# ScalarE evacuates the adaLN product banks, M6 becomes the last product of a feed-forward, and a fifth load buffer replaces two slots

## The chip, the cores and the metric

One core of a Trainium2 chip runs the whole kernel. The metric is the device time of one execution in microseconds; lower is better. The times shown are of several executions, and one further execution was recorded by the hardware profiler.

## The reference

A trunk of two layers over 512 tokens with 1024 channels. Each layer has three sub-layers: a SwiGLU feed-forward, a token mixer (mLSTM in layer 0, Mamba-2 in layer 1) and a second feed-forward. Every sub-layer is wrapped in the same way, with a shift, a scale and a gate that come from a conditioning vector (adaLN):

```python
def swiglu(h, w1, w3, w2):
    return (jax.nn.silu(h @ w1) * (h @ w3)) @ w2

def sublayer(x, fn, g_pre, g_post, shift, scale, gate, weight):
    hmod = rms_norm(x, g_pre) * (1 + scale[:, None, :]) + shift[:, None, :]
    y = rms_norm(fn(hmod), g_post)
    return x + weight * gate[:, None, :] * y

# per layer i
mod = (c_act @ ada_w[i] + ada_b[i]).reshape(B, N_SUB, 3, D_MODEL)
```

All of it is float32, and d_ff is 2816 (22 tiles of 128).

## The kernel before, in words

**Products in three matmuls.** TensorE multiplies in a reduced float32 format, so each operand is split into a high part (ScalarE copy, L174 or L191) and a low part (VectorE subtraction, L175 or L192), and each product is three matmuls (`mm3`, L186 to L188).

**Loads.** Weights come through `raw` tiles of 128x1024 floats from the pool `rawp`, which has four buffers. SyncE issues these loads in order. A `raw` is free again when its low part has been computed, which in turn writes into one of three `wl` buffers, whose reader is TensorE. Loads of weights stand on L162 (`unit`), of adaLN's weights on L203, of the feed-forward's second matrix on L713 (`blocks`), and of pieces for the late products on L723 (`behind`).

**Slots.** All other activations live in 52 tiles of 128x512 floats (`Slots`), taken first freed, first used. A taken slot carries a wait for the last reader of what it held. A `raw` buffer is as large as two slots. Counted through the program, the fewest free slots at any `get` are 3, at the end of three of the feed-forwards (names `kl`, `v`, and once `grow` in the first of them); in the Mamba mixer the fewest are 4.

**Feed-forward.** `first` and `rest` run over the 22 tiles of d_ff; each tile is two projections into PSUM banks `mm0` and `mm1`, silu on ScalarE (L598) and a product on VectorE (L599). Pairs of tiles give factors for a fast (Strassen-like) second product with seven half-size products M1 to M7. `flush` runs M5, M1 and M7 as the stream goes, and stores three combinations of weight blocks to DRAM from GpSimd (`w2s`, L688). `outp` then runs M3, M4, and two rows of token tiles last: before, M6 and then M2, the last three groups of which are kept in slots (`hold`, L191 and L192) so that one token tile ends before the other. M6 enters one half (`hi`) of the rows of token tiles 2 and 3, M2 enters both halves, one of them subtracted. `Post.evac` squares and gates a half, `Post.finish` does the norm, the residual and the next sub-layer's input (or, after the last sub-layer, the store of the output).

**adaLN beside it.** In the streams of the feed-forwards, `pump` runs steps of adaLN: a load of 128x1024 weights and a multiply-add on VectorE (L208). When a sum is ready, `settle` runs `columns` (shift and scale: 24 narrow matmuls, bank read at L233) or `gate_rows` (gate: two matmuls at L252 for each of two halves, bank read by VectorE at L254, which also adds the row loaded at L249). They take an `aux` bank if one is free and otherwise an `mm` bank in turn; all six `gate_rows` of the program take `mm0` and `mm1`, the same that the next tile of the stream needs. VectorE and ScalarE each run their instructions in one order, laid out when the kernel is built.

Of the kernel before, what the change touches and what calls it, by code (L numbers as in the profile page):

```python
# [12 lines left out]
AF = mybir.ActivationFunctionType  # L13
ALU = mybir.AluOpType
# [4 lines left out]
ND = D // P  # L19
# [16 lines left out]
HELD = 3  # L36
# [11 lines left out]
START_A = 1  # L48
START_X = (2,3)
START_S = 4  # L50
N_SLOTS = 52
ADA_END = 20
ADA_R = (2.6,2.25,2.25,1)

# [2 lines left out]
def trunk(ctx: ExitStack, tc: tile.TileContext, i: dict, out: bass.AP):  # L57
    nc = tc.nc
    pool = lambda name, bufs=1, **k: ctx.enter_context(tc.tile_pool(name=name, bufs=bufs, **k))
# [2 lines left out]
    hmp = pool("hmp", 16)  # L62
    ygp = pool("ygp", 4)
    slp = pool("slp")
    rawp = pool("rawp", 4)
    whp = pool("whp", 3)
    wlp = pool("wlp", 3)
    accp = pool("accp", 1)
# [4 lines left out]
    act = nc.scalar.activation  # L73
    tt = nc.vector.tensor_tensor
# [20 lines left out]

    slots, banks = Slots(slp, "s", N_SLOTS), Slots(aux, "a", 4)

    def slot(dt=F32, name="sl", cols=T):
        return slots.get(dt, name, cols)
# [5 lines left out]
    def ps_mm(k=None):  # L105

        if k is None:
            k = mm_turn[mm_next[0] % len(mm_turn)]
            mm_next[0] += 1
        return mm.tile([P, T], F32, tag=f"mm{k}", name="mm")  # L110

    def ps_aux():
        return banks.get(F32, "aux")
# [3 lines left out]
    def ps_ada():  # L117

        if banks.free_:
            ps = ps_aux()  # L120
            return ps, lambda: done_ps(ps)
        return ps_mm(), lambda: None


    def load_const(name):
        ap = i[name]
        t = const.tile(list(ap.shape), F32, name="c_" + name)
        nc.sync.dma_start(t, ap)
        return t
# [5 lines left out]
    ada_b = load_const("ada_b")  # L135
# [48 lines left out]
    def mm3(ps, stat, mov, first, last):  # L184

        matmul(ps, stat[0], mov[0], start=first, stop=False)  # L186
        matmul(ps, stat[0], mov[1], start=False, stop=False)  # L187
        matmul(ps, stat[1], mov[0], start=False, stop=last)  # L188

    def split(dst_h, dst_l, src):  # L190
        act(dst_h, src, AF.Copy)  # L191
        tt(dst_l, src, dst_h.bitcast(F32), ALU.subtract)  # L192
# [5 lines left out]
    def ada_kind(l, s, kind):  # L198
        st = {}

        def step(kc):
            raw = rawp.tile([P, 1024], F32, tag="raw", name="raw")
            nc.sync.dma_start(raw, i["ada_w"][l * 9 + s * 3 + kind - 2, kc])  # L203
            if kc == 0:
                st["acc"] = accp.tile([P, 1024], F32, tag="acc", name="acc")
                ts(st["acc"], raw, csil[:, 0:1], None, ALU.mult)
            else:
                stt(st["acc"], raw, csil[:, kc:kc + 1], st["acc"], ALU.mult, ALU.add)  # L208
            if kc == ND - 1:
                acc = st["acc"]  # L210
                if kind == 2:
                    parts = []
                    for c in range(2):
                        parts.append((slot(F32R, "adah"), slot(F32R, "adal")))
                        split(*parts[c], acc[:, c * T:(c + 1) * T])
                    ready.append(lambda: gate_rows(parts))
                else:
                    parts = [slot(BF16, "adas", 1024) for _ in range(3)]
                    act(parts[0], acc, AF.Copy)
                    tt(acc, acc, parts[0], ALU.subtract)  # L220
                    act(parts[1], acc, AF.Copy)
                    tt(parts[2], acc, parts[1], ALU.subtract)
                    ready.append(lambda: columns(parts))

        def columns(parts):
            ps, done = ps_ada()
            for j in range(ND):
                for q in range(3):
                    matmul(ps[:, j:j + 1], parts[q][:, j * P:(j + 1) * P], ones_b, start=q == 0, stop=q == 2)
            n0 = (l * 3 + s) * ND  # L230
            c0 = kind * DEPTH * NSUB * ND + n0
            r = const.tile([P, ND], F32, name=f"mod{l}{s}{kind}")
            tt(r, ps[:, :ND], ada_b[:, c0:c0 + ND], ALU.add)  # L233
            free(*parts)
            done()
            if kind == 0:
                SH[l, s] = r
            else:
                stt(r, r, 1.0, n_pre[:, n0:n0 + ND], ALU.add, ALU.mult)
                A[l, s] = r  # L240

        def gate_rows(parts):

            G[l, s] = []
            for c in range(2):
                rows = []
                for name in ("gate_b", "norm_post"):
                    rows.append(slot(name="row"))
                    nc.sync.dma_start(rows[-1], i[name][l * 3 + s:l * 3 + s + 1, c * T:(c + 1) * T].to_broadcast([P, T]))  # L249
                ps, done = ps_ada()  # L250
                for q, t in enumerate(parts[c]):
                    matmul(ps, ones_r, t, start=q == 0, stop=q == 1)  # L252
                g = slot(name="grow")
                tt(g, ps, rows[0], ALU.add)  # L254
                stt(g, g, 0.5 if s != 1 else 1.0, rows[1], ALU.mult, ALU.mult)
                G[l, s].append(g)
                free(*rows, *parts[c])
                done()
        for kc in range(ND):
            adaq.append(lambda kc=kc: step(kc))  # L260

# [271 lines left out]
    class Ffn:  # L533
# [207 lines left out]
        def outp(self, nxt):  # L741
            n = NF // 2
            groups = [range(j, min(j + 2, n)) for j in range(0, n, 2)]
            lo, hi = slice(0, T), slice(T, D)
            m3 = [ps_mm(0), ps_mm(1)]
            for js in groups[:3]:
                self.sums(m3, 3, js)
            while self.pairs or self.pending:
                self.step()
            post = Post(self.l, self.sub, nxt)  # L750
            m, yg = self.m, post.yg
            for t in range(2):
                act(yg[2 + t][:, hi], m[1][t], AF.Copy)
                act(yg[t][:, hi], m[5][t], AF.Copy)
                tt(yg[t][:, lo], yg[2 + t][:, hi], m[7][t], ALU.add)
                tt(yg[t][:, lo], yg[t][:, lo], yg[t][:, hi], ALU.add)
            done_ps(*m[1], *m[5])
            for js in groups[3:]:
                self.sums(m3, 3, js)
            for t in range(2):  # L760
                tt(yg[t][:, hi], m3[t], yg[t][:, hi], ALU.subtract)
                tt(yg[2 + t][:, hi], yg[2 + t][:, hi], m3[t], ALU.add)
                post.evac(t, 1, yg[t][:, hi])

            m4 = [ps_aux(), ps_aux()]
            for js in groups:
                self.sums(m4, 4, js)
                for j in js:
                    free(*self.kept[j]["34"])
            for t in range(2):  # L770
                tt(yg[t][:, lo], yg[t][:, lo], m4[t], ALU.add)
                act(yg[2 + t][:, lo], m4[t], AF.Copy)
            done_ps(*m4)
            for t in range(2):
                post.evac(t, 0, yg[t][:, lo])
                post.finish(t)

            m6 = [ps_mm(2), ps_mm(3)]
            for js in groups:
                self.sums(m6, 6, js)  # L780
            for t in range(2):
                tt(yg[2 + t][:, hi], yg[2 + t][:, hi], m6[t], ALU.add)

            m2, held = [ps_mm(0), ps_mm(1)], {}
            for js in groups[:-HELD]:
                self.sums(m2, 2, js)
                for j in js:
                    free(*self.kept[j]["62"])
            for js in groups[-HELD:]:
                held.update(zip(js, self.hold(2, js)))  # L790
            for t in range(2):
                c = slice(t * P, (t + 1) * P)
                for j in held:
                    ah, al = self.kept[j][2]
                    mm3(m2[t], (ah[:, c], al[:, c]), held[j], False, j == n - 1)
                    if t:
                        free(*self.kept[j]["62"], *held[j])
                u = 2 + t
                tt(yg[u][:, lo], yg[u][:, lo], m2[t], ALU.add)
                post.evac(u, 0, yg[u][:, lo])  # L800
                tt(yg[u][:, hi], yg[u][:, hi], m2[t], ALU.subtract)
                post.evac(u, 1, yg[u][:, hi])
                post.finish(u)
            mm_turn[:] = [0, 1, 2, 3]
            return post
# [472 lines left out]
    ps = [[ps_mm(), ps_mm()], [ps_mm(), ps_mm()], p2]  # L1278
# [46 lines left out]
    post = f00.outp((0, 1))  # L1325
# [18 lines left out]
    post = Post(0, 1, (0, 2))  # L1344
# [3 lines left out]
    post = f01.outp((1, 0))  # L1348
# [3 lines left out]
    post = f10.outp((1, 1))  # L1352
# [19 lines left out]
    post = Post(1, 1, (1, 2), mb.yacc)  # L1372
# [91 lines left out]
```

## Time and profile before

| | us |
|---|---|
| median of three runs | 2104.86 |
| the three runs | 2102.46 to 2107.49 |
| the profiled execution, its own time | 2103.91 |
| the profiled execution, span from first to last instruction | 2102.1 |

TensorE is busy for 2043.4 us of the span (97%), VectorE for 1618.5 (77%), ScalarE for 1004.0 (48%), GpSimd for 83.2 (4%). The mean granted clock of TensorE is 0.993 of full speed. A busy TensorE is no proof that it runs at its peak: the granted clock of a stretch says at which of its two levels (1.2 and 2.4 GHz) it ran, 1.00 being all of it at the higher. In an idle row, the name behind the arrow is what the engine waited for last.

### The profile page before, as it was taken

The page shows a single profiled execution, that of the slowest core. Times are in us where ns is not written, and L with a number is a line of the kernel's source. Part 1 is how long each engine was busy: PE and PEld are TensorE (multiplying, and loading weights), DVE is VectorE, ACT ScalarE, POOL GpSimd, SP SyncE. Part 2 cuts the span into 40 slices and gives each one's busy share as a digit, 9 for nine tenths or more (in the row PEclk, how much of TensorE's full clock was granted, in tenths as well). Part 3 has the DMA queues.
Part 4 walks back from the last instruction along what each step waited for, and adds up shares of the span by engine and source line. Part 5 has one row for each costly group of instructions (what it writes and reads, how often), then busy time and mean ns, then how long its engine had stood idle before and what let it go on. Part 6 is the DMA issues. An engine that isn't in the chain of part 4 may idle for free.

```text
span 2102.1 us, 28333 instructions
## 1 busy us (share of the span) xinstructions
PE 2043.4 (97%) x10422; PEld 1704.5 (81%) x10422; DVE 1618.5 (77%) x2687; ACT 1004.0 (48%) x1721; POOL 83.2 (4%) x165
## 2 busy tenths in 40 slices
PE   7999999999999999899999999999999999999998
PEld 5887778898789788788977788888887789878886
DVE  8979977858986888668768787889898758575666
ACT  5434335645564343347533334765665645333344
POOL 0001000000000000000000000000000000000000
PEclk9999999999999999999999999999999999999999
DMA  7567775445424677745467675533433334454454
GB/s 275 184 200 244 261 244 187 137 146 157 138 79 156 204 262 243 229 153 173 156 221 264 211 232 180 168 127 118 131 96 120 121 111 131 165 180 147 157 163 155
DMA packets 124604, 369.17 MB, mean 176 GB/s; under 512 B 15081, under 2 KB 15081, under 8 KB 124465
## 3 DMA queue, kind: packets, MB, share of 16 engines
q1 hardware_dynamic: 113904, 332.75, 49.4%
q0 software_dynamic: 10560, 34.61, 4.3%
q8 instruction: 81, 1.33, 0.3%
q14 instruction: 59, 0.48, 0.1%
HBM read 330.46 MB, written 36.85 MB: 175 GB/s over the span
## 4 chain that ended last, share of the span: by engine, by line
issue 48%; PE 34%; DVE 8%; DMA 6%; ACT 3%; POOL 1%; SPq 0%; POOLq 0%; DVEq 0%; ACTq 0%
PE mm L186 9%; PE mm L188 9%; PE mm L187 9%; DMA raw<-in_w 3%; PE aux L186 2%; PE aux L188 2%; PE aux L187 2%; DMA raw<-in_ada_w 2%; DVE wl L192 1%; POOL w2s L688 1%; DVE wl L175 1%; ACT wh L174 1%; DVE acc L208 1%; DVE tl L192 0%; DVE kl L192 0%
## 5 line engine op out<-in xcount | busy, mean ns | idle before, releaser
L186 PE MATMUL mm<-hm,wh 128*128 128x512 f32 (+1 forms) x2128 | 775.4, 367 | 13.1 <-DVE grow L254 6.6
L188 PE MATMUL mm<-hm,wl 128*128 128x512 f32 (+1 forms) x2128 | 772.1, 364 | 11.2 <-DVE wl L175 11.2
L187 PE MATMUL mm<-hm,wh 128*128 128x512 f32 (+1 forms) x2128 | 773.0, 364 | 0.0
L186 PEld LDWEIGHTS mm<-hm,wh 128*128 128x128 f32 x2128 | 402.7, 190 | 81.5 <-ACT wh L174 9.8
L188 PEld LDWEIGHTS mm<-hm,wl 128*128 128x128 f32 x2128 | 403.9, 190 | 78.7 <-DVE wl L175 16.4
L187 PEld LDWEIGHTS mm<-hm,wh 128*128 128x128 f32 x2128 | 404.4, 190 | 61.9 <-issue 2.0
L174 ACT ACTIVATE wh<-raw 128x1024 fp32r<-128x1024 f32 (+1 forms) x294 | 278.3, 957 | 360.1 <-PE mm L187 125.5
L175 DVE TENSOR_TENSOR wl<-raw,wh 128x1024 fp32r<-128x1024 f32 (+1 forms) x294 | 319.3, 1098 | 88.1 <-ACT wh L174 85.4
L191 ACT ACTIVATE wh<-raw 128x1024 fp32r<-128x1024 f32 (+1 forms) x172 | 158.2, 920 | 281.0 <-PE mm L187 146.4
L192 DVE TENSOR_TENSOR wl<-raw,wh 128x1024 fp32r<-128x1024 f32 (+1 forms) x172 | 179.9, 1048 | 50.4 <-ACT wh L191 49.0
L208 DVE SCALAR_TENSOR_TENSOR acc<-raw,csil,acc 128x1024 f32<-128x1024 f32 x112 | 143.8, 1284 | 75.3 <-DMA raw<-in_ada_w 74.9
L599 DVE TENSOR_TENSOR s<-s,mm 128x512 f32<-128x512 f32 (+1 forms) x97 | 59.8, 619 | 87.4 <-PE mm L188 87.1
L191 ACT ACTIVATE kh<-s 128x256 fp32r<-128x256 f32 x132 | 54.4, 412 | 86.0 <-DVE s L599 75.5
L186 PE MATMUL mm<-wh,kh 128*128 128x512 f32 x224 | 87.7, 392 | 0.0
L187 PE MATMUL mm<-wl,kh 128*128 128x512 f32 x224 | 87.5, 391 | 0.0
L188 PE MATMUL mm<-wh,kl 128*128 128x512 f32 x224 | 87.3, 390 | 0.0
L688 POOL DMA_DIRECT2D w2s<-v x44 | 24.0, 546 | 1392.9 <-DVE v L680 922.2
L186 PE MATMUL aux<-wh,th 128*128 128x512 f32 x176 | 68.6, 391 | 0.9 <-ACT wh L191 0.8
L187 PE MATMUL aux<-wl,th 128*128 128x512 f32 x176 | 68.4, 390 | 0.5 <-DVE wl L192 0.5
L188 PE MATMUL aux<-wh,tl 128*128 128x512 f32 x176 | 68.3, 389 | 0.0
L680 DVE TENSOR_TENSOR v<-raw 128x512 f32<-128x512 f32 x44 | 30.3, 690 | 41.3 <-DMA raw<-in_w 41.0
L191 ACT ACTIVATE th<-traw 128x256 fp32r<-128x256 f32 x88 | 35.9, 410 | 53.7 <-DVE traw L634 46.2
(313 smaller groups left out, 3088.7 us busy)
## 6 DMA issues: line engine op xcount, KB each, us to landing
raw<-in_w SPq DMA_DIRECT2D x278, 512.0 KB, 4.3
raw<-in_ada_w SPq DMA_DIRECT2D x128, 512.0 KB, 4.3
raw<-w2s SPq DMA_DIRECT2D x60, 512.0 KB, 3.6
raw<-in_mb_wx SPq DMA_DIRECT2D x24, 512.0 KB, 3.8
w2s<-v POOLq DMA_DIRECT2D x44, 256.0 KB, 3.3
w2s<-u POOLq DMA_DIRECT2D x44, 256.0 KB, 3.2
w2s<-raw POOLq DMA_DIRECT2D x44, 256.0 KB, 2.6
a<-in_ada SPq DMA_DIRECT2D x32, 256.0 KB, 5.4
```

What stands on the lines that cost most here:

```text
L174: act(hi[:, :b - a], raw[:, a:b], AF.Copy)
L175: tt(lo[:, :b - a], raw[:, a:b], hi[:, :b - a].bitcast(F32), ALU.subtract)
L186: matmul(ps, stat[0], mov[0], start=first, stop=False)
L187: matmul(ps, stat[0], mov[1], start=False, stop=False)
L188: matmul(ps, stat[1], mov[0], start=False, stop=last)
L191: act(dst_h, src, AF.Copy)
L192: tt(dst_l, src, dst_h.bitcast(F32), ALU.subtract)
L208: stt(st["acc"], raw, csil[:, kc:kc + 1], st["acc"], ALU.mult, ALU.add)
L599: tt(s[:, a:b], s[:, a:b], p[1][:, a:b], ALU.mult)
L680: tt(v, r0[:, lo], r0[:, hi], ALU.add)
L688: nc.gpsimd.dma_start(self.pre[m, j // 2][j % 2], src)
```

## The change

Three things are changed.

- The pool `rawp` gets five buffers in place of four, and the number of slots goes from 52 to 50.
- In `columns` and `gate_rows` ScalarE copies the bank to SBUF, the bank is handed back, and VectorE then adds the bias in SBUF, in place. VectorE issues as many instructions as before; ScalarE issues 22 more (10 of 128x8, 12 of 128x512).
- At the end of each feed-forward M2 comes before M6. M2's bank pair is now `mm2`, `mm3` and M6's `mm0`, `mm1`; the kept last groups are M6's. The half `lo` of token tiles 2 and 3 is squared and gated behind M2, and only `hi` behind M6.

```diff
-N_SLOTS = 52
+N_SLOTS = 50
...
-    rawp = pool("rawp", 4)
+    rawp = pool("rawp", 5)
...
-            tt(r, ps[:, :ND], ada_b[:, c0:c0 + ND], ALU.add)
+            act(r, ps[:, :ND], AF.Copy)
+            done()
+            tt(r, r, ada_b[:, c0:c0 + ND], ALU.add)
             free(*parts)
-            done()
...
-                tt(g, ps, rows[0], ALU.add)
+                act(g, ps, AF.Copy)
+                done()
+                tt(g, g, rows[0], ALU.add)
                 stt(g, g, 0.5 if s != 1 else 1.0, rows[1], ALU.mult, ALU.mult)
                 G[l, s].append(g)
                 free(*rows, *parts[c])
-                done()
...
-            m6 = [ps_mm(2), ps_mm(3)]
+            m2 = [ps_mm(2), ps_mm(3)]
             for js in groups:
+                self.sums(m2, 2, js)
+            for t in range(2):
+                u = 2 + t
+                tt(yg[u][:, lo], yg[u][:, lo], m2[t], ALU.add)
+                tt(yg[u][:, hi], yg[u][:, hi], m2[t], ALU.subtract)
+                post.evac(u, 0, yg[u][:, lo])
+
+            m6, held = [ps_mm(0), ps_mm(1)], {}
+            for js in groups[:-HELD]:
                 self.sums(m6, 6, js)
-            for t in range(2):
-                tt(yg[2 + t][:, hi], yg[2 + t][:, hi], m6[t], ALU.add)
-
-            m2, held = [ps_mm(0), ps_mm(1)], {}
-            for js in groups[:-HELD]:
-                self.sums(m2, 2, js)
                 for j in js:
                     free(*self.kept[j]["62"])
             for js in groups[-HELD:]:
-                held.update(zip(js, self.hold(2, js)))
+                held.update(zip(js, self.hold(6, js)))
...
                 u = 2 + t
-                tt(yg[u][:, lo], yg[u][:, lo], m2[t], ALU.add)
-                post.evac(u, 0, yg[u][:, lo])
-                tt(yg[u][:, hi], yg[u][:, hi], m2[t], ALU.subtract)
+                tt(yg[u][:, hi], yg[u][:, hi], m6[t], ALU.add)
                 post.evac(u, 1, yg[u][:, hi])
                 post.finish(u)
```

## Rows read from the trace of the kernel before

**Rows 1.** The page's first part: each engine's busy time, share of span, instructions.
```profile
PE 2043.4 (97%) x10422; PEld 1704.5 (81%) x10422; DVE 1618.5 (77%) x2687; ACT 1004.0 (48%) x1721; POOL 83.2 (4%) x165
```
**Rows 2.** By stretch: PE, PEld, DVE, ACT, POOL busy, clock, DMA share, GB/s.
```profile
0.00:25.00 25.00, 10.10 (x37) 7.73 (x38) 15.95 (x60) 16.88 (x31) 1.99 (x9) 1.00 0.91 333
...
275.00:300.00 25.00, 22.32 (x91) 17.73 (x90) 18.35 (x23) 7.28 (x10) 2.17 (x4) 0.93 0.80 274
...
725.00:750.00 25.00, 22.85 (x92) 18.05 (x92) 19.77 (x29) 6.69 (x11) 1.63 (x3) 0.93 0.61 215
...
850.00:875.00 25.00, 22.87 (x94) 18.52 (x93) 19.69 (x30) 9.34 (x16) 1.62 (x3) 0.93 0.71 221
875.00:900.00 25.00, 21.74 (x83) 17.40 (x83) 16.90 (x22) 6.14 (x9) 1.62 (x3) 0.86 0.59 200
...
1150.00:1175.00 25.00, 22.22 (x88) 17.50 (x88) 19.82 (x31) 7.62 (x13) 1.08 (x3) 0.90 0.70 232
```
**Rows 3.** Waits of PE, whole span: total us, times, longest.
```profile
PE mm L186 <- DVE grow L254: 6.6, 5, 3.3
```
**Rows 4.** Waits of PE within streams 150:325, 700:925, 1075:1300 and 1825:2025.
```profile
PE mm L186 <- ACT wh L174: 3.7, 4, 2.2
PE mm L188 <- DVE wl L175: 2.8, 5, 0.7
...
PE mm L188 <- DVE wl L175: 2.3, 2, 2.1
...
PE mm L188 <- DVE wl L175: 1.6, 2, 0.9
...
PE mm L188 <- DVE wl L175: 3.2, 2, 2.9
```
**Rows 5.** Waits of SyncE's DMA queue, whole span: total us, times, longest.
```profile
SPq L162 <- DVE wl L175: 473.3, 123, 24.6
```
**Rows 6.** SyncE and VectorE in order of time, 1855 to 1870 us.
```profile
1860.49 1.46 SPq L713 DMA_DIRECT2D raw<-in_w  x2
...
1866.58 0.69 DVE L679 TENSOR_TENSOR u<-raw 128x512 f32<-128x512 f32 x1 [0.59 <-DMA raw<-in_w]
...
1869.00 1.22 DVE L175 TENSOR_TENSOR wl<-raw,wh 128x1024 fp32r<-128x1024 f32 x1
```
**Rows 7.** PE, VectorE and ScalarE in order of time, 876 to 890 us.
```profile
880.29 0.39 PE L252 MATMUL mm<-adal,ones_r 128*128 128x512 f32 x1
883.94 0.77 PE L186 MATMUL mm<-hm,wh 128*128 128x512 f32 x1 [3.26 <-DVE grow L254]
...
883.11 1.28 DVE L254 TENSOR_TENSOR grow<-mm,row 128x512 f32<-128x512 f32 x2
...
884.31 1.06 ACT L174 ACTIVATE wh<-raw 128x1024 fp32r<-128x1024 f32 x1 [5.08 <-DMA raw<-in_w]
```
**Rows 8.** PE before the next tile, 308 to 318 us.
```profile
314.48 0.47 PE L186 MATMUL mm<-hm,wh 128*128 128x512 f32 x1 [0.41 <-DVE grow L254]
```
**Rows 9.** Line 598, ScalarE reading a bank: ns min, median, max.
```profile
L598 ACT ACTIVATE s<-mm x97: 364/578/600, 77.9 to 2023.3; 128x512 f32<-128x512 f32 x73, 128x256 f32<-128x256 f32 x24
```
**Rows 10.** PE, VectorE and ScalarE in order of time, 2076 us to the end.
```profile
2091.74 0.39 PE L188 MATMUL mm<-bh,kl 128*128 128x512 f32 x1
...
2088.76 0.69 DVE L799 TENSOR_TENSOR yg<-yg,mm 128x512 f32<-128x512 f32 x1 [5.37 <-PE mm L188]
...
2093.54 1.41 DVE L469 SCALAR_TENSOR_TENSOR x<-yg,rc,x 128x512 f32<-128x512 f32 x2
...
2096.06 0.21 DVE L309 TENSOR_SCALAR rc<-ssq 128x1 f32<-128x1 f32 x1
...
2093.65 0.63 ACT L458 ACTIVATE sq<-yg 128x512 f32<-128x512 f32 x1
```
**Rows 11.** Page's part 6, a store of GpSimd: KB each, us to landing.
```profile
w2s<-v POOLq DMA_DIRECT2D x44, 256.0 KB, 3.3
```
**Rows 12.** Waits of SyncE's DMA queue within 1480 to 1700 us.
```profile
SPq L834 <- DVE cv L1070: 11.7, 3, 4.3
```

More of the change, by code (lines that the diff above doesn't have):

```diff
@@ L793, in outp @@
                 for j in held:
-                    ah, al = self.kept[j][2]
-                    mm3(m2[t], (ah[:, c], al[:, c]), held[j], False, j == n - 1)
+                    ah, al = self.kept[j][6]
+                    mm3(m6[t], (ah[:, c], al[:, c]), held[j], False, j == n - 1)
                     if t:
```

## The prediction

> **What bounds the kernel now.** I read the page's first part before anything else: TensorE is busy for 97% of the span, so only what it stands still for, or runs slowly for, can be won [rows 1]. 2102.1 less 2043.4 is 58.7 us of idle. The view by stretches of 25 us says where. The first stretch has 14.9 us of it [rows 2], and behind the last matmul, 2092.1 to the end, lie 10.0 [rows 10]; that leaves 34 us inside. A stretch at full pace is busy throughout at a granted clock of 1.00; 875 to 900 is idle for 3.3 us and has a clock of 0.86 [rows 2]. So a gap costs twice: once as idle, and again because part of the stretch behind it runs at the lower of the two clock levels. 25 x (1 - 0.86) = 3.5 us is that second price there. Over the stretches with a lowered clock in the four feed-forward streams (275, 725, 850, 875 and 1150) it is 1.75 + 1.75 + 1.75 + 3.5 + 2.5 = 11 us [rows 2].
>
> Next, the waits of TensorE. Two kinds fill the streams. It waits for the gate's bank to be read by VectorE at L254: 6.6 us in five gaps, the longest 3.3 [rows 3]. And it waits for the split of a weight just loaded: 3.7 + 2.8 in the first stream, 2.3, 1.6 and 3.2 in the others, 13.6 us [rows 4]. The order of time shows what lies behind each. At 1866 VectorE stands first for a block of the second matrix whose load SyncE issued at 1860.5 to 1862; the low part that TensorE needs is queued behind and starts at 1869.0 [rows 6]. And SyncE issues late because it waits for a `raw` buffer: its largest wait by far is for the low parts that free one, 473 us in 123 waits [rows 5]. At 880 TensorE has given the last gate matmul by 880.7, and VectorE comes to L254 only at 883.11, behind other work in its order; TensorE goes on at 883.94. ScalarE stands idle for 5.08 us over that same time [rows 7].
>
> **The change part by part.** The sum is made against the profiled execution's own 2103.9 us, 1.8 above its span; the median of the runs is 1.0 above that, and I add it at the end.
>
> *M6 last, at the end of the program.* The last matmul starts at 2091.74 and the last norm starts at 2096.06 (L309). Between them VectorE adds and subtracts M2, ScalarE squares twice and VectorE gates twice, with the other tile's residual of 1.41 between. Then 6.0 us follow to the end at 2102.1, which don't change [rows 10]. With M6 last, one half is left per tile. The first tile's matmuls end at about 2088.7; its add takes 0.69, its square 0.63 with 0.2 for the reading of the sum, the norm's small steps about 0.9 (by the same steps before), and its residual 1.41, so VectorE is through with it at about 2092.6. Then the last tile's add (0.7), square and read-out (0.8): L309 at about 2094.1 in place of 2096.06, **-1.9 us**. If the residual is ordered behind the add it is -2.3; if the other way it stays -1.9. In the four other places the same edit makes the next input ready a little earlier; TensorE has other work there, so I take 0 (from -2 to +1: four more VectorE operations fall together behind M2, while it also splits M6's first weights).
>
> *ScalarE reads the gate's bank.* ScalarE gets 12 copies of 128x512 at about 0.58 us, the duration of its read of the same size from a bank [rows 9], and 10 tiny ones: 7 us in all beside 1004 of 2102 busy, off the path. VectorE's own count is unchanged, and no stretch waits for the columns' bank, so that half is worth nothing. The gain is what TensorE waits for L254: 6.6 us, and with it its share of the clock's price: 3.5 behind the gap at 880, half of 1.75 at 725, half of 2.5 at 1150, together 5.6. Not all can go. Where VectorE stood free, the wait was still 0.41 [rows 8], since the next tile needs the bank at once and a copy by ScalarE takes about as long as the add. Six places x 0.41 = 2.5 stays. Best: 6.6 + 5.6 - 2.5 = -9.7. Worst: the copy is behind a split that waits for its load. At the place in rows 7 it would then end at 884.31 + 1.06 + 0.58 = 885.95 in place of about 883.8, 2.2 later; six such places make +13. ScalarE is idle in most of the windows and VectorE isn't, so I lie nearer to the gain: **-5**. By the Trainium skill ("TensorE: Matmul & The Clock Gate", the table at its head) ScalarE's queue is a strict FIFO; that is a rule against this part, and the idle of 5.08 us before a split agrees with it. By that rule alone the worst case would hold wherever the built order puts the split first; the third rival has it.
>
> *The fifth buffer.* Nothing is removed or added in work; each load may be issued one load earlier. In the stream from 700 on, 227 GB/s, less the stores, is a load of 512 KB each 2.5 us or so (an estimate from the rates of its stretches, 200 to 221 [rows 2]). The gaps for a split are each at most 2.9 [rows 4], so one load earlier could close nearly all: 13.6 us, and the clock behind them (1.75 at 275, half of 1.75 at 725, 1.75 at 850), 4.4: best -18. It is 0 if what stands late is the order on VectorE or the DMA engines' rate. Many of the gaps are short ones of about 0.5 that lie between high and low part of one weight, and one load earlier shortens the wait for the first alone. I take half, **-9**. For the rate: the streams move 200 to 274 GB/s at a DMA share of 0.59 to 0.80, and the first stretch shows 333 at 0.91 [rows 2], so there is room. By the Trainium skill ("DMA: Bandwidth & Descriptors", Specifications) memory gives one core about 358 GB/s; that leaves an estimated quarter free in the densest stretch, and no run here shows the figure itself.
>
> *Two slots fewer.* Where 3 were free, 1 is: at the end of three of the feed-forwards a `kh`, `kl` or `v` takes the slot just freed, whose last reader may be a store of GpSimd, 3.3 us to landing [rows 11]. ScalarE or VectorE then stands there, and the splits and silu behind it in its order with it. In the Mamba mixer the broadcast rows (L834) take slots on SyncE's queue, which already waits up to 4.3 us for one [rows 12], and the weight loads are queued behind. Cover: by then the products M1, M5, M7 and M3 have work for TensorE. From 0 to +20 (below); I take **+2**.
>
> *All of it is laid out anew* when built: each edit shifts orders on every engine. I count that as some us of spread with no sign.
>
> Sum: 2103.9 - 1.9 - 5 - 9 + 2 = 2090; with the median's 1.0, **2091 us**.
>
> **The rivals.**
> 1. *Loads were not the limit.* The fifth buffer fills, and VectorE's order keeps the low parts where they are. For: VectorE is 77% busy and the rows at 1866 show a low part behind other work; against: that other work itself waited for a load. 2104.9 - 1.9 - 5 + 2 = **2100**.
> 2. *The change doesn't do what it says: the gate's copy is late on ScalarE too.* Half the places lose 2.2 each (+6.5), loads win: 2104.9 - 1.9 - 9 + 2 + 6.5 = **2102.5**. For: 5.08 us of ScalarE standing for a load at just such a place [rows 7].
> 3. *Slots decide, slower.* At four ends of feed-forwards an engine stands for the store of a slot just freed, 3.3 us, nothing covers it and the clock falls behind it as at 850 (1.75): 4 x 5.05 = +20. With the gate's gain and the tail, and no gain of loads, since the loads wait for the same engine: 2104.9 - 1.9 - 5 + 20 = 2118; with the loads' half gain **2109**. It decides from about +20 on, that is, if every end pays in full. Against: three free slots before, and no wait of TensorE for any of these now.
>
> **How the numbers follow.** About 0.2%, 4.2 us, is what a measurement of this kernel tells from no change. The forecast, 2091 with a range of its own from 2083 to 2099, has 0.58, nearly all of it faster. Rival 1 has 0.20, split about the line at 2100.6. Rival 2 has 0.09, mostly no change. Rival 3 has 0.13, mostly slower. That gives 0.64 faster, 0.22 the same, 0.14 slower. The range goes from 2081 (best gate and a third more of the loads) to 2107 (rivals 1 and 2 in full, and the lower part of rival 3).
>
> **What would show it.** In the profile after: no wait of TensorE for L254, and waits of some 0.4 for the new copy; waits for the weight splits in the four streams at half of 13.6 or less; granted clock 1.00 at the stretches that had 0.86 and 0.93; from the last matmul's start to the last norm's start (L309) some 2.4 us where 4.3 were [rows 10]. The prediction is wrong if SyncE's waits fall but TensorE's don't (rival 1), if TensorE's wait for the copy exceeds 6.6 (rival 2), or if waits for `kh`, `kl`, `s` or `bc` appear that were not there (rival 3).

## The result and the profile after

The changed kernel took 2081.34 us (median of four runs, 2077.22 to 2083.75), beside 2104.78 for the kernel before: a ratio of 0.9888, with a 95% interval from 0.9872 to 0.9904. That is 23.4 us faster, clear of the 4.2 us that count as no change. The forecast was 2091 with a range from 2081 to 2107, so the sign held, and the gain was larger than forecast by 10 us. The time lies outside the forecast's own range (2083 to 2099) and 0.3 us inside the lower end of the wide one.

The first part of the page after, engine busy time, share of the span and instructions, to be read beside [rows 1]:

```profile
PE 2035.2 (98%) x10422; PEld 1701.5 (82%) x10422; DVE 1619.0 (78%) x2687; ACT 1013.6 (49%) x1743; POOL 82.2 (4%) x165
```

The span is 2078.8 us, so TensorE is idle for 43.6 us where it was 58.7, 15.1 less. Its mean granted clock rose from 0.993 to 0.997, which over the span is another 8.3 us (0.004 x 2079). Together they make the 23.3 us by which the spans differ. The engines do the same work; ScalarE has its 22 instructions and 9.6 us more.

Where in the program? I cut both executions at the last residual of each sub-layer. The first feed-forward with the start takes 394.3 us in place of 405.5, the fourth sub-layer's feed-forward 360.1 in place of 368.1, and the last to the end 349.5 in place of 353.9. The second feed-forward gains only 1.1 (371.1 for 372.2), Mamba 1.4, and the mLSTM stage loses 2.8 (227.1 for 224.3). So the gain lies in the feed-forwards that stream adaLN's weights beside their own, above all in the first and the fourth sub-layer's. TensorE's waits there, by stretches 150:325, 700:925 (the next three lines), 1075:1300 and 1825:2025, beside [rows 4]:

```profile
PE mm L186 <- ACT grow L255: 0.7, 1, 0.7
PE mm L188 <- DVE wl L175: 0.2, 1, 0.2
...
PE mm L186 <- DVE s L601: 2.7, 1, 2.7
PE mm L188 <- DVE wl L175: 1.1, 2, 0.7
...
PE mm L188 <- DVE wl L175: 0.9, 1, 0.9
PE mm L186 <- ACT grow L255: 0.8, 1, 0.8
```

The waits for the split of a weight, 13.6 us before, are 2.2. The gate's bank (now L255, read by ScalarE) costs 0.7 to 0.8 at each of four places, 2.9 in all, for the 6.6 of [rows 3]. One new wait stands out, 2.7 us for `s` at L601, the reading of a product bank. Four stretches of the after kernel, columns as in [rows 2]:

```profile
775.00:800.00 25.00, 22.29 (x109) 18.00 (x108) 19.18 (x27) 9.58 (x15) 1.62 (x3) 0.86 0.72 240
...
875.00:900.00 25.00, 25.00 (x112) 20.71 (x111) 15.82 (x27) 9.72 (x16) 1.08 (x2) 1.00 0.41 134
...
950.00:975.00 25.00, 22.55 (x106) 17.88 (x104) 22.99 (x45) 19.37 (x37) 0.00 (x0) 1.00 0.54 178
975.00:1000.00 25.00, 24.78 (x177) 23.47 (x178) 23.17 (x50) 20.09 (x34) 0.00 (x0) 0.93 0.65 205
```

The clock of 0.86 at 875 is gone, and one of 0.86 has come at 775, behind the gap of 2.7. That takes back part of what the second feed-forward gains: one place was mended, another opened. The rest goes at its end, where M6 now comes last: 2.45 us of idle at 950 to 975 and a clock of 0.93 behind it, where the kernel before has at most 0.3 of idle in a stretch there and 1.00. Without M6 last (a run below) this feed-forward takes 367.1 us, though it has a gap of 3.4 at the same place near 788. The order of time there:

```profile
786.40 0.69 DVE L682 TENSOR_TENSOR v<-raw 128x512 f32<-128x512 f32 x1 [0.65 <-DMA raw<-in_w]
787.01 1.22 DVE L175 TENSOR_TENSOR wl<-raw,wh 128x1024 fp32r<-128x1024 f32 x1
788.15 0.68 DVE L601 TENSOR_TENSOR s<-s,mm 128x512 f32<-128x512 f32 x1
...
786.71 0.16 ACT L233 ACTIVATE mod<-mm 128x8 f32<-128x8 f32 x1
...
788.97 0.77 PE L186 MATMUL mm<-hm,wh 128*128 128x512 f32 x1 [2.71 <-DVE s L601]
```

VectorE works through a step of adaLN's split, two splits of weights and a block of the second matrix, for whose load it stands 0.65, before it reads the product bank at L601, and the next tile needs that bank. ScalarE had read the bank of the shift and scale at 786.71, 2 us earlier.

### The profile page after: what moved, and what is told of

Read it like the earlier page. It is cut to its first block, busy times and chain, and to the rows that moved or that the text cites. A ratio compares the mean times of both kernels' runs of the same rounds, so it can differ in the third digit from the quotient of the medians.

```text
span 2078.8 us, 28340 instructions
## 1 busy us (share of the span) xinstructions
PE 2035.2 (98%) x10422; PEld 1701.5 (82%) x10422; DVE 1619.0 (78%) x2687; ACT 1013.6 (49%) x1743; POOL 82.2 (4%) x165
## 4 chain that ended last, share of the span: by engine, by line
PE 71%; DVE 10%; DMA 8%; issue 6%; ACT 3%; POOL 0%; SPq 0%; DVEq 0%; POOLq 0%; ACTq 0%
PE mm L186 20%; PE mm L188 20%; PE mm L187 19%; DMA raw<-in_w 4%; PE aux L186 3%; PE aux L187 3%; PE aux L188 3%; DMA raw<-in_ada_w 2%; DVE wl L175 2%; DVE acc L208 1%; ACT wh L174 1%; PE aux L1177 1%; DVE wl L192 1%; PE aux L1188 1%; PE aux L1142 1%
## 5 line engine op out<-in xcount | busy, mean ns | idle before, releaser
L174 ACT ACTIVATE wh<-raw 128x1024 fp32r<-128x1024 f32 (+1 forms) x294 | 278.2, 957 | 355.3 <-PE mm L187 159.0
L601 DVE TENSOR_TENSOR s<-s,mm 128x512 f32<-128x512 f32 (+1 forms) x97 | 59.8, 618 | 98.9 <-PE mm L188 93.0
L600 ACT ACTIVATE s<-mm 128x512 f32<-128x512 f32 (+1 forms) x97 | 51.3, 531 | 22.1 <-PE mm L188 22.0
```

The lines of the kernel that those rows point to most:

```text
L174: act(hi[:, :b - a], raw[:, a:b], AF.Copy)
L600: act(s[:, a:b], p[0][:, a:b], AF.Silu)
L601: tt(s[:, a:b], s[:, a:b], p[1][:, a:b], ALU.mult)
```

## The experiments

Each was timed beside runs of the kernel before on the same chip, which had medians of 2104.3 to 2104.7. Ratios are to those.

**One part at a time.** The fifth buffer with 50 slots, nothing else:

```diff
-N_SLOTS = 52
+N_SLOTS = 50
...
-    rawp = pool("rawp", 4)
+    rawp = pool("rawp", 5)
```

> Only the pool of loads (five buffers, 50 slots); bank reads and product order as before. Theory (the loads' wait is the larger part, and the parts add): TensorE's waits for weight splits in the four streams fall from 13.6 us to under 4, the clock dips at 275 and 850 go, and the 6.6 us for L254 stay; some 12 us faster than before, about 2093. Rival (the loads matter only beside the freed banks): under 5 us faster, about 2100 or more. Rival (slots cost): waits for kh, kl, s or bc show up, and it is no faster.

Measured: 2085.89 us, ratio 0.9909 (0.9891 to 0.9927), 18.4 us faster. The loads' part alone carries most of the change. The waits of TensorE in this kernel, whole span:

```profile
PE mm L186 <- DVE grow L254: 3.6, 5, 1.6
PE mm L188 <- DVE wl L175: 3.2, 5, 1.3
PE mm L186 <- DVE mod L233: 2.9, 1, 2.9
```

Two things here were not expected. The wait for the gate's bank fell from 6.6 to 3.6 though VectorE still reads it. And a wait of 2.9 us appeared for the bank of the shift and scale (L233), which had none before. It is the gap that the whole change has near 788:

```profile
790.70 0.68 DVE L599 TENSOR_TENSOR s<-s,mm 128x512 f32<-128x512 f32 x1
791.29 0.16 DVE L233 TENSOR_TENSOR mod<-mm,c_ada_b 128x8 f32<-128x8 f32 x1
...
791.52 0.77 PE L186 MATMUL mm<-hm,wh 128*128 128x512 f32 x1 [2.85 <-DVE mod L233]
```

VectorE reads the product bank (L599) and, directly behind, the small one (L233, 0.16 us). TensorE goes on 0.14 us after the end of the product's reading, here and in the whole change (L601, 788.15 + 0.68 to 788.97). So L233 gives the wait its name and adds nothing to it.

ScalarE's reading of the banks, nothing else (four load buffers, 52 slots):

```diff
-            tt(r, ps[:, :ND], ada_b[:, c0:c0 + ND], ALU.add)
+            act(r, ps[:, :ND], AF.Copy)
+            done()
+            tt(r, r, ada_b[:, c0:c0 + ND], ALU.add)
             free(*parts)
-            done()
...
-                tt(g, ps, rows[0], ALU.add)
+                act(g, ps, AF.Copy)
+                done()
+                tt(g, g, rows[0], ALU.add)
...
-                done()
```

> Only ScalarE's reading of the adaLN banks; four load buffers, 52 slots, product order as before. Theory: the wait for the gate's bank falls from 6.6 us to about 3 (0.7 at each of four places), and the lowered clock behind 880 goes; the waits for the splits stay at 10 to 16; some 6 us faster, about 2099. Rival (the gate is late on ScalarE too, or the stall moves to the next load): within 3 us of before, 2102 or more.

Measured: 2098.48, ratio 0.9975 (0.9958 to 0.9992), 5.8 us faster. Its waits of TensorE, whole span:

```profile
PE mm L188 <- DVE wl L175: 9.4, 10, 2.4
PE mm L186 <- ACT wh L174: 6.9, 6, 2.2
...
PE mm L186 <- ACT grow L255: 2.8, 4, 1.1
```

The gate's wait is 2.8 for 6.6, and the waits for the splits stay, as the theory has it. In the stream of [rows 7] the wait for the gate is 0.2, and no clock is lost behind it.

M6 last, nothing else (the last two hunks of the diff ahead):

> Only the order of M2 and M6. Theory: from the start of the last matmul to the end of the span 0.7 us less than before (10.4), and nothing to speak of elsewhere: 2103 to 2105. Rival (the earlier halves let the next sub-layer start sooner, four times): 4 us or more faster, 2100 or less, with fewer waits around the ends of the feed-forwards.

Measured: 2109.21, ratio 1.0020 (1.0006 to 1.0035), 4.9 us slower. Both expectations missed. Its waits of TensorE, whole span:

```profile
PE mm L186 <- DVE grow L254: 8.3, 5, 5.0
...
PE mm L187 <- DVE bl L192: 3.6, 3, 1.9
```

The second line is the edit's own: TensorE waits for the low part of the first kept group, up to 1.9 us where the longest was 0.3 before, since more of VectorE's work now stands behind M2, just ahead of that split. The first line is in a stream that the edit doesn't touch. Its 5.0 is the place of [rows 7], where VectorE comes to L254 through the same instructions as before, but had stood longer for a load of adaLN's weights, 3.92 us for 3.10 (before's line stands below, under the fifth buffer):

```profile
876.83 1.29 DVE L208 SCALAR_TENSOR_TENSOR acc<-raw,csil,acc 128x1024 f32<-128x1024 f32 x1 [3.92 <-DMA raw<-in_ada_w]
```

The profiled execution was the fastest of its twelve (2104.2), so the lines say where time goes, not the whole 4.9.

ScalarE's reading and M6 last together, four load buffers:

> ScalarE's reading and M6 last together, with four load buffers and 52 slots. Theory (parts add): the two effects in sum, about 7 us faster, 2098; the waits for splits in the streams at 10 us or more. Rival (the parts need each other): nearer to 2085, the fifth buffer being worth little once banks are free.

Measured: 2103.92, ratio 0.9992 (0.9978 to 1.0005). The single parts' -5.8 and +4.9 make -0.9, measured -0.4: within the intervals they add. Without the fifth buffer the rest of the change is worth nothing that can be measured.

**With the fifth buffer.** The change without M6 last:

> The whole change but the order of M2 and M6. Theory (M6 last costs, loads and banks win and add): -19.2 and -5.3 of the single parts make 2080, level with or a little below the whole change at 2081.3; no wait of 1.3 for bl at the end of the second feed-forward. Rival (M6 last earns its place once loads are early): 2084 or more.

Measured: 2081.41, ratio 0.9891 (0.9873 to 0.9909): no different from the whole change. (The expectation counts with -19.2 and -5.3 where the medians above give -18.4 and -5.8; the sum is 2080 with either.) The change without ScalarE's reading:

> The whole change but ScalarE's reading of the banks. Theory (parts add): -19.2 and +4.9 make 2090, and the waits for the banks read by VectorE (L233, L254 of before) stay at 4 us or more. Rival (M6 last costs only where loads are late, so not here): 2085 or less.

Measured: 2082.86, ratio 0.9905 (0.9885 to 0.9925), where the sum of the parts is 2090.8. So beside the fifth buffer M6 last shows no cost in the whole (2085.89 to 2082.86 without the banks' edit, 2081.41 to 2081.34 with it), and ScalarE's reading brings 4.5 without M6 last and 1.5 with it. Each of these medians has an interval of 3.4 to 4.2 us to either side, so none of the differences is clear of it. In the profiled executions the second feed-forward is longer with M6 last in all four pairs, by 2.8 and 5.5 us with four buffers and by 3.4 and 4.0 with five, so its cost there stays; what the other stages do differs from pair to pair, and why is not shown. In this kernel TensorE waits for the banks that VectorE reads:

```profile
PE mm L186 <- DVE mod L233: 4.4, 1, 4.4
PE mm L186 <- DVE grow L254: 4.2, 5, 1.5
```

ScalarE's reading makes 2.9 of the second in the whole change. The first is again the gap near 788, and taking L233 from VectorE does not remove it: the kernels in which ScalarE reads the bank have 2.7 to 5.0 there, put down to the product bank's reading (L601 in the whole change).

**The two slots.**

> Only 50 slots in place of 52; four load buffers. It prices the two slots by themselves. Theory: +0 to +3, 2104 to 2107, no new wait of TensorE above 1 us. Rival (slots decide): +8 or more with waits for kh, kl, s or bc, which the fifth buffer would then have outweighed.

Measured: 2110.64, ratio 1.0028 (1.0013 to 1.0043), 5.9 us slower, between the two expectations. TensorE has no wait for `kh`, `kl` or `bc`, and neither ScalarE nor VectorE has one for a store of GpSimd; the longest waits, the start's aside, are for other lines (`s` at L599 is the reading of a product bank):

```profile
PE mm L188 <- DVE wl L175: 10.6, 12, 1.7
PE mm L186 <- ACT wh L174: 5.8, 4, 3.4
PE mm L252 <- DVE s L599: 3.7, 2, 3.0
```

By stages of the profiled execution (the second fastest of twelve, 2104.63) the first feed-forward is 2.7 us shorter than before and the second 5.0 longer, where free slots are equally few. That speaks against a price by slot, as far as one execution can. The whole change with 51 slots, the room taken from the start's diagonal tiles, tests it from the other side:

```diff
-N_SLOTS = 50
+N_SLOTS = 51
...
-            self.diag.append(const.tile([P, P], F32, name=f"diag{t}"))
+            if t == 0:
+                self.diags = slot(name="diags")
+            self.diag.append(self.diags[:, t * P:(t + 1) * P])
```

> The whole change with 51 slots, the room for one of them from the start's diagonal tiles, which move into a slot. Theory (the +5.9 of 50 slots alone was a new order of the whole program and not a wait for slots): within 4 us of the whole change, with no sign, 2077 to 2085. Rival (each slot costs 3 us): 2078 or less, and 1.3 us for bl at the end of the second feed-forward gone.

Measured: 2080.81, ratio 0.9892 (0.9879 to 0.9905): no different from the whole change, and the wait of 1.3 for `bl` is still there. With five buffers the 51st slot brings nothing that shows. What makes 50 slots slower with four buffers is open.

**How many buffers.** Three in the kernel before:

```diff
-    rawp = pool("rawp", 4)
+    rawp = pool("rawp", 3)
```

> The kernel before with three load buffers in place of four, 52 slots. It measures the step below. Theory (a load's lateness sets the streams' gaps, so the price grows as buffers go): 30 us or more slower, 2135 or above, with waits for weight splits in the streams at 30 us or more against 13.6, and more lowered clock. Rival (the fifth buffer's gain came from a new order of work and not from loads): within 10 us of before.

Measured: 2150.76, ratio 1.0221 (1.0199 to 1.0242), 46 us slower. Waits of TensorE, and two of the streams by stretches:

```profile
PE mm L186 <- ACT wh L174: 28.7, 15, 4.6
PE mm L186 <- DVE grow L254: 15.0, 6, 4.6
...
150.00:325.00 175.00, 156.05 (x679) 123.94 (x678) 138.69 (x213) 63.19 (x104) 14.13 (x26) 0.94 0.69 226
700.00:925.00 225.00, 208.44 (x908) 166.68 (x907) 165.75 (x236) 75.31 (x118) 13.04 (x24) 0.95 0.67 218
```

Late loads raise the gate's wait too, from 6.6 to 15.0, with no edit there, and the clock of the first stream sinks to 0.94. Six in the whole change (the diagonal tiles and the Mamba mask moved into slots to make room):

```diff
-    rawp = pool("rawp", 5)
+    rawp = pool("rawp", 6)
...
-    mask = const.tile([P, T], F32, name="mask")
+    mask = slot(name="mask")
```

> The whole change with six load buffers and 50 slots; the room comes from the start's diagonal tiles and the Mamba mask, which move from constants into slots. Theory (five buffers have closed nearly all gaps of loads: 2.5 us of waits for splits are left in the whole program): no more than 4 us faster, 2077 to 2085. Rival (the streams still run on loads): 8 us or more faster, 2073 or less.

Measured: 2094.97, ratio 0.9957 (0.9943 to 0.9972): 13.6 us slower than with five, and neither theory had that. Its waits of TensorE, and the order of time at the longest (in this kernel L170 is the low part, L183 its matmul, L678 to L683 the second matrix's sums):

```profile
PE mm L183 <- DVE wl L170: 12.9, 11, 2.4
...
215.33 1.06 ACT L169 ACTIVATE wh<-raw 128x1024 fp32r<-128x1024 f32 x1 [0.52 <-PE aux L183]
...
212.71 0.69 DVE L679 TENSOR_TENSOR v<-raw 128x512 f32<-128x512 f32 x1 [2.83 <-DMA raw<-in_w]
...
220.19 2.35 DVE L170 TENSOR_TENSOR wl<-raw,wh 128x1024 fp32r<-128x1024 f32 x2
...
221.46 0.79 PE L183 MATMUL mm<-hm,wl 128*128 128x512 f32 x1 [2.41 <-DVE wl L170]
```

The high part is done by 216.4, so the load of that weight is early. VectorE stood 2.83 for a block of the second matrix and then does its batch in the order laid out; the low parts come at 220.2. At this place it is as the first rival of the prediction has it: VectorE's order decides. But the loads are not early everywhere. VectorE stands 158 us for adaLN's loads and the second matrix's in the whole program (73.2, 46.1 and 39.0), 120 with five buffers and 150 in the kernel before. Why a sixth buffer makes these later is not shown; the two tiles that moved changed the layout too. Of the 15.7 us by which the spans of six and five differ, 7.1 lie in the first feed-forward and 7.6 in the fourth sub-layer's, and only 2.0 in Mamba, where the mask is used.

**The tail.** The whole change, with the gated halves of token tiles 2 and 3 at the end of the program written to slots of their own:

```diff
-            tt(self.yg[t][:, cs], src, self.grow[c], ALU.mult)
+            if self.nxt is None and t >= 2:
+                self.gated[t, c] = slot(name="gy")
+                tt(self.gated[t, c], src, self.grow[c], ALU.mult)
+            else:
+                tt(self.yg[t][:, cs], src, self.grow[c], ALU.mult)
...
-                    stt(x[t][:, cs], self.yg[t][:, cs], r, x[t][:, cs], ALU.mult, ALU.add)
+                    y = self.gated.get((t, c), self.yg[t][:, cs])
+                    stt(x[t][:, cs], y, r, x[t][:, cs], ALU.mult, ALU.add)
```

> The whole change, and at the end of the program the gated halves of token tiles 2 and 3 go to slots of their own, so that VectorE needn't wait for ScalarE's square of the same tile. It tests why the tail gained 0.7 us and not the 1.9 forecast. Theory (the in-place product waits for the square, once in each of the two tiles): from the start of the last matmul to the end of the span 8.2 us in place of 9.4; 0.79 of idle before L461 is gone twice. Rival (the norm's small steps and the store set the tail): 9.4 stays.

Measured, from the start of the last matmul to the end of the span: 2072.36 to 2080.6, 8.24 us, as the theory has it. The tail of the change, and then of this kernel:

```profile
2069.41 0.39 PE L188 MATMUL mm<-bh,kl 128*128 128x512 f32 x1
...
2072.45 0.69 DVE L461 TENSOR_TENSOR yg<-yg,grow 128x512 f32<-128x512 f32 x1 [0.79 <-ACT sq L460]
2073.06 0.21 DVE L311 TENSOR_SCALAR rc<-ssq 128x1 f32<-128x1 f32 x1
```

```profile
2072.36 0.39 PE L188 MATMUL mm<-bh,kl 128*128 128x512 f32 x1
...
2074.05 0.69 DVE L464 TENSOR_TENSOR gy<-yg,grow 128x512 f32<-128x512 f32 x1
2074.80 0.21 DVE L311 TENSOR_SCALAR rc<-ssq 128x1 f32<-128x1 f32 x1
```

The idle of 0.79 before the gating is gone, and the last norm starts 2.44 us after the start of the last matmul, as the prediction had it (2.4), where the whole change has 3.65. Yet the kernel took 2084.53, ratio 0.9911 (0.9893 to 0.9929), no faster than the whole change: the gain of 1.1 us is smaller than the scatter, and the order of the work is another one from the mLSTM stage on, though the edit stands at the end.

**An edit without a mechanism.** Only the ten tiny copies of the shift and scale, in the kernel before:

> The kernel before with ScalarE reading the bank of the shift and scale alone (ten tiny copies); the gate's bank stays with VectorE. No wait of TensorE for L233 stands in the trace before, so by mechanism it is worth 0. Theory (any edit lays the orders anew, and that alone moves the time by several us): up to 6 us off before to either side, 2098 to 2110, with other gaps at other places. Rival (the order is stable and single parts can be read to a microsecond): within 2 us of before.

Measured: 2105.88, ratio 1.0009 (0.9995 to 1.0023). The median stays within 2 us, as the rival has it, so laying the orders anew was not by itself worth 6 here. In its profiled execution the gaps are at other places all the same (the first feed-forward 3.2 us shorter, the fourth sub-layer's 2.0 longer).

## Why the prediction was right, and where its sizes were not

**What bounds the kernel: right.** All of the gain is idle and lowered clock of TensorE (15.1 and 8.3 us), nearly all in the streams, and a gap cost twice where it was long, as the new one at 788 shows. That the time lies inside the range is partly luck: the terms for the buffer and its slots were 11 us too small together, and the time lies below the forecast's own range, in the last 2 us of the wide one. Of the signs named, the clock is 1.00 at all the stretches that had 0.86 and 0.93 in the streams, and the waits for splits are far below half. A wait for `s` has come, the third rival's sign, but for another reason: it is the reading of the product bank at L601, behind VectorE's order, and no slot.

**The fifth buffer: right in mechanism, too small.** The term was -9 with +2 for the slots, and the two measured -18.4 together. The step that was off is "I take half", and before it the sum of the best case at -18, slots not counted. It counted only the gaps that the trace put down to a split. With four buffers and three, the wait for L254 moved with the loads too (15.0, 6.6, 3.6 for three, four, five buffers, VectorE reading the bank in all three). The order of time of the kernel before shows why. Ahead of three of its four longest gaps in the streams VectorE had stood for a load of adaLN's weights, and what TensorE needs, a low part or the reading of the gate's bank, comes behind it in VectorE's order (the third of the gaps is the one at 883.94 in [rows 7]):

```profile
849.43 1.28 DVE L208 SCALAR_TENSOR_TENSOR acc<-raw,csil,acc 128x1024 f32<-128x1024 f32 x1 [6.25 <-DMA raw<-in_ada_w]
...
852.50 0.79 PE L188 MATMUL mm<-hm,wl 128*128 128x512 f32 x1 [2.13 <-DVE wl L175]
...
1858.04 1.28 DVE L208 SCALAR_TENSOR_TENSOR acc<-raw,csil,acc 128x1024 f32<-128x1024 f32 x1 [4.17 <-DMA raw<-in_ada_w]
1859.24 2.35 DVE L175 TENSOR_TENSOR wl<-raw,wh 128x1024 fp32r<-128x1024 f32 x2
...
1860.52 0.50 PE L188 MATMUL mm<-hm,wl 128*128 128x512 f32 x1 [2.91 <-DVE wl L175]
...
875.95 1.28 DVE L208 SCALAR_TENSOR_TENSOR acc<-raw,csil,acc 128x1024 f32<-128x1024 f32 x1 [3.10 <-DMA raw<-in_ada_w]
```

The place that the prediction read for this, 1866 to 1869 [rows 6], is not one: TensorE has no gap behind it, and the 2.9 of that stream had ended at 1860.52. Over the whole program VectorE's idle time before adaLN's multiply-adds falls from 75 us to 42, here as groups of before and after, while its waits for the second matrix's loads do not fall (76 and 78):

```profile
L208 DVE SCALAR_TENSOR_TENSOR acc<-raw,csil,acc 128x1024 f32<-128x1024 f32 x112 | 143.8, 1284 | 75.3 <-DMA raw<-in_ada_w 74.9
```

```profile
L208 DVE SCALAR_TENSOR_TENSOR acc<-raw,csil,acc 128x1024 f32<-128x1024 f32 x112 | 143.5, 1281 | 42.9 <-DMA raw<-in_ada_w 41.9
```

So one cause stood behind two rows of waits, and halving each was the error. The doubt about short gaps between high and low part was wrong as well: of 13.6 us (14.4 with a wait of 0.8 for L174 in the third stream, which that sum leaves out), 2.2 are left. By the Trainium skill ("DMA: Bandwidth & Descriptors", Specifications) a core has about 358 GB/s of memory; with five buffers the densest 25 us of a stream moved 289 GB/s (288 before, more than the 274 that the prediction names), and the first stretch 333, so there was room, as argued. No trace here shows the figure itself.

**ScalarE's reading: -5 forecast, -5.8 measured alone** (-1.7 to -8.8 by the interval). The size was right for four buffers. The wait that stays was put at 0.41 in six places, 2.5 us, and is 0.7 to 0.8 in four of them, 2.9. At each of the four a split of 1.06 stands directly before the copy, one of them in the first three lines here; where ScalarE was free, at 880 in the run with its reading alone (the last line), the wait was 0.23:

```profile
870.23 1.06 ACT L174 ACTIVATE wh<-raw 128x1024 fp32r<-128x1024 f32 x1 [1.61 <-PE mm L188]
871.19 1.07 ACT L255 ACTIVATE grow<-mm 128x512 f32<-128x512 f32 x2
871.82 0.50 PE L186 MATMUL mm<-hm,wh 128*128 128x512 f32 x1 [0.70 <-ACT grow L255]
```

```profile
880.15 0.50 PE L186 MATMUL mm<-hm,wh 128*128 128x512 f32 x1 [0.23 <-ACT grow L255]
```

That agrees with the strict order of ScalarE's queue, which the Trainium skill states ("TensorE: Matmul & The Clock Gate", the table at its head); it cost some 0.5 us at each of the four places (an estimate, 0.70 to 0.75 less 0.23). The second rival, a copy stuck behind a split that stands for its load, is refuted in its price: the worst wait for the copy is 0.8 in the whole change and 1.1 alone. (The prediction's "the third rival has it" means this one, the second.) That the columns' half is worth nothing was not refuted: the waits for L233 at five buffers are a gap that stays when ScalarE reads that bank.

**M6 last: -1.9 in the tail forecast, -0.7 measured there** (4.3 to 3.65 from the start of the last matmul to the last norm; 10.4 to 9.4, so -1.0, to the end). The step that failed is that the gate's product runs beside the square. It writes in place over what ScalarE still reads, and waits 0.79, once per tile; the run with slots of its own shows it (8.24). In the other places 0 was taken from a range of -2 to +1; with four buffers the edit cost 4.9 on the whole, outside that range, and with five no cost shows in the whole. The wait for `bl` of up to 1.9 is its own, and the second feed-forward is longer with it in every pair of executions; the rest of the 4.9 isn't placed.

**Slots: +2 forecast; +5.9 with four buffers, and nothing that shows with five.** The mechanism given, an engine standing for the store that last read a slot, appears in the trace of neither 50 slots alone nor the whole change, so the third rival is refuted as told, and the price of 50 slots in the kernel before is left unexplained.

**Rival 1** (VectorE's order, not loads) fell for five buffers. At six a place can be seen where that order holds TensorE up, but loads are late there as well, so it is not shown to be the bound.

## What to carry to other kernels

When in-order engines stand first in line for loads, a late load is booked under many names: price the buffer by all waits that share the engine, not by the rows that name the load. One buffer fewer shows whether loads set the pace (46 us for the fourth), but not what the next one is worth: here the fifth brought 18 and a sixth, with two tiles moved for it, took 14 back, so the number is to be measured, not raised. And a wait bears the name of what came last. When that reader was moved to another engine (the columns' bank, near 788), the wait took the next reader's name and stayed.

## What the runs showed of the hardware that was not expected

The same program scatters by up to 0.8% between executions on one chip: seventeen runs of the kernel before lay from 2093.7 us at a mean granted clock of 0.997 to 2111.3 at 0.993 (and 2110.1 at 0.990), with a median of 2104.7. Two other groups of its runs spread by 8 us (seventeen) and 12 (twenty-nine). The kernels with five buffers spread by 4 to 7 us in four to six runs each, too few to call it less. A profile of one execution can therefore sit 5 us beside its kernel's median, as with M6 last alone (2104.2 beside 2109.2), and a difference of a few us between two traces is read only with the timed runs beside it.
